# Transposing the attention's probabilities with VectorE and a pass through HBM instead of with TensorE

## The chip, the core and the metric

The kernel runs on one core of a Trainium2 chip. The core has a matrix engine (TensorE, PE in the profile, with its weight loads as PEld), three engines for elementwise work (VectorE or DVE, ScalarE or ACT, GpSimd or POOL), a queue that issues transfers (SyncE or SP) and 16 DMA engines that move data between HBM and the on-chip memory SBUF. SBUF has 128 partitions. TensorE writes to a second memory, PSUM, which has eight banks of 128 x 512 fp32. The metric is the device time of one execution in microseconds, lower is better.

## The reference: what is computed

One decoder block on 512 positions of 1024 channels, in fp32. A combined projection feeds a gated short convolution and an attention; both are merged with two gates, projected and added to the input; a gated FFN with a convolution follows.

```
h   = rmsnorm(x);  P = h @ w_in
yA  = B * causal_dwconv3(C * x_in)
yB  = attention(q, compressed / selected / window keys)     # 8 heads of 64, 2 key groups
x   = x + ( sigmoid(gA) * (yA @ W_A) + sigmoid(gB) * (yB @ W_B) ) @ W_o
x   = x + ( silu(conv3(W_g rmsnorm(x)) + b) * (W_u rmsnorm(x)) ) @ W_down
```

The attention is what matters here. For a block of 128 queries, each head has three softmaxes: over at most 31 compressed keys, over the selected blocks and over a window. With 512 positions there are 8 blocks of 64 keys and up to 16 may be selected, so all are; the window is 512 long. The last two are thus both plain causal attention, over different keys and values:

```
p   = softmax(where(key <= query, q . k * scale, -1e30))
out = g0 * (p_cmp @ v_cmp) + g1 * (p_sel @ v_sel) + g2 * (p_win @ v_win)
```

## The kernel before

All products run in a fast fp32 form (F32R) that keeps fewer bits, so each factor is split into a high and a low part, and a product takes three matmuls (high x high, high x low, low x high). `dense` (lines 408 to 414) does this for the weight tiles: one tile of 128 output channels takes 8 x 3 matmuls of 128x512.

The stages are: the token projections (q, keys, values), the heads (norm and rotary embedding), the compressed keys, the attention, then the convolution tiles `conv_tile` (12 weight tiles, PSUM name pa), the gate tiles `gate_tile` (16, pg), the mixing of the convolution `mix_a_pair` (pma), the mixing of the attention (pmb), the output projection w_o, and the FFN. A planner puts the instructions of each engine in an order of its own, by a timeline that it works out ahead of the run from dependencies, program order and its own costs. What depends on nothing in the attention (pa, pg, pma) is therefore mixed into it. The order of each engine and of each DMA queue is fixed by the time the kernel runs; each instruction waits for its inputs and its buffers.

The attention is `attend(pt_, g, qt)`, lines 595 to 708, called for the query tiles 3, 2, 1, 0 and the groups 0, 1 (lines 789 to 791). Query tile qt sees qt + 1 key tiles of 128. Per branch (br 1 is the window, br 0 the selected keys) and for four heads:

- Two matmuls give the scores of a head, 128 queries on the partitions, keys along the row (lines 608, 609). VectorE adds the causal mask to the last tile (657) and takes the negated maximum (658). ScalarE writes the exponential to `e` and sums it (659).
- VectorE makes 1/sum times the branch's gate (612, 613), and ScalarE scales the four rows of `e` by it (663). For query tile 0 both branches share one `e`, and one VectorE instruction scales it (644).
- The product with the values needs the keys on the partitions. For each key tile, TensorE transposes four 128x128 squares of `e`, one per head, into a PSUM bank `pt` (687). ScalarE rounds the bank to its high part `ph` (690), VectorE subtracts to the low part `pl` (691), and two matmuls add to the accumulator `po` (693, 698).
- With br 0 come the compressed keys: their small softmax (667 to 676, two steps of it on GpSimd, 672 and 673), two transposes (679) and two matmuls (697).
- The accumulator is read out (700, 705), split in two and stored for pmb (707, 708).

A branch of a group and query tile, or for query tile 0 both branches together, is called a turn below; there are 14. The buffers: three tiles `e` of 128x2048 (NE), three each of `ph` and `pl` (NPT), two PSUM banks for `pt`, one for `po`.

Weights come by transfers on the queue of SP, into rings. For pg and pma, `load_w` (lines 125 to 137) loads a raw tile (wr, three buffers), ScalarE makes the high part (134) and GpSimd the low part (136). The attention's tiles lie in pools that are closed after it (802); the pool for the weights of pmb takes their place (805), so the loads of w_bo (172) wait for the attention's end.

Of the kernel before, what the change touches and what calls it, by code (L numbers as in the profile page):

```python
# [18 lines left out]
P = 128  # L19
D = 1024  # L20
S = 512
# [25 lines left out]
NWF = 3  # L47
NE = 3
NWU = 11
QT_ORDER = (3, 2, 1, 0)  # L50
NPT = 3
NF_T = 10
# [30 lines left out]
def tile_block(ctx: ExitStack, tc: tile.TileContext, xT, pos, par, par2, w_tok, w_a3, w_gate, w_ao, w_bo, w_o,  # L83
               w_ff, w_dn, c_w1, out):
    nc = tc.nc
    sb = ctx.enter_context(tc.tile_pool(name="sb", bufs=1, side="left"))
    ps = ctx.enter_context(tc.tile_pool(name="ps", bufs=1, space=bass.MemoryType.PSUM))
    pxg = ctx.enter_context(tc.tile_pool(name="pxg", bufs=1, side="left"))
# [501 lines left out]
    def y_tile(i):  # L590
        if i // 2 not in y_all:
            y_all[i // 2] = pa.tile([P, 4 * TOKC], F32R, name=f"y{i // 2}", tag=f"y{i // 2}", bufs=1)
        return y_all[i // 2][:, 4 * S * (i % 2):4 * S * (i % 2 + 1)].rearrange("p (a s) -> p a s", a=4)

    def attend(pt_, g, qt):
        nk = (qt + 1) * P
# [5 lines left out]
        def small(name, n, dt=F32):  # L602
            pool = pxg if name in ("mx1", "mx0", "sums1") else pb if name in ("sums0", "mcs") else pt_
            return pool.tile([P, HG, n], dt, name=f"{name}{tag}", tag=name, bufs=2)

        def scores(w, i, br, a, b):
# [9 lines left out]
        if off == 0:  # L616
# [5 lines left out]
            nc.vector.tensor_add(xc, xc, pcm[:, :, NC:2 * NC])  # L622
        acc = o_bank(f"po{tag}")
        if qt == 0:

            e = pt_.tile([P, HG, S], F32, name=f"e{tag}", tag="e", bufs=NE)[:, :, 0:2 * P]
            e4 = e.rearrange("p h (b k) -> p h b k", b=2)
            mx = pt_.tile([P, HG, 2], F32, name=f"mx{tag}", tag="mx", bufs=1)
            sums = small("sums", 2)
            for i in range(HG):  # L630
# [8 lines left out]
                for br in (1, 0):  # L639
                    nc.scalar.activation(e4[:, i, br], dg[:, br], AF.Exp, bias=mx[:, i, br:br + 1],  # L640
                                         accum_out=sums[:, i, br:br + 1])
            nc.vector.reciprocal(sums, sums)
            nc.vector.tensor_mul(sums, sums, gates[:, :, 1:3])
            nc.vector.tensor_tensor(e4, e4, sums[:, :, :, None].to_broadcast([P, HG, 2, P]), op=ALU.mult)
        for br in (1, 0):
            if qt > 0:
                o = off if br == 0 else 0
                e = pt_.tile([P, HG, S], F32, name=f"e{tag}{br}", tag="e", bufs=NE)
                mx = small(f"mx{br}", 1)
                sums = small(f"sums{br}", 1)  # L650
                for i in range(HG):
                    sc = s_bank(f"sc{tag}{i}{br}")
                    scores(sc[:, 0:o + nk], i, br, NC - o, NC + nk)
                    if o:
                        nc.vector.tensor_add(xc[:, i, :], sc[:, 0:NC], cm_add[:, qt, :])
                    dg = sc[:, o + nk - P:o + nk]
                    nc.vector.tensor_add(dg, dg, causal)
                    nc.vector.tensor_reduce(mx[:, i], sc[:, o:o + nk], axis=AX.X, op=ALU.max, negate=True)
                    nc.scalar.activation(e[:, i, 0:nk], sc[:, o:o + nk], AF.Exp, bias=mx[:, i], accum_out=sums[:, i])
                scale_of(sums, 1 + br)  # L660
                for i in range(HG):
                    v = e[:, i, 0:nk]
                    nc.scalar.activation(v, v, AF.Copy, scale=sums[:, i])
            if br == 0:
                mcs = small("mcs", 2)
# [18 lines left out]
            for kt in range(qt + 1):  # L684
                pt = t_bank(f"pt{tag}{kt}{br}")
                for i in range(HG):
                    nc.tensor.transpose(pt[:, i * P:(i + 1) * P], e[:, i, (kt + k0) * P:(kt + k0 + 1) * P], ident)  # L687
# [3 lines left out]
                nc.vector.tensor_sub(pl, pt, ph.bitcast(F32))  # L691
                w = v_t[:, kt, 2 * br + g, :]
                nc.tensor.matmul(acc, w, ph, start=kt == 0 and br == 1, stop=False)
                if kt == 0 and br == 0:
                    a4 = acc.rearrange("p (a b t) -> p a b t", a=2, b=2)
                    for b in range(2):
                        nc.tensor.matmul(a4[:, :, b], vc_t[:, b, g, :], pc, start=False, stop=False)
                nc.tensor.matmul(acc, w, pl, start=False, stop=kt == qt and br == 0)
# [3 lines left out]
        av = acc[0:HD, :].rearrange("p (a b t) -> p a b t", a=2, b=2)  # L702
        tv = tmp.rearrange("p (a b t) -> p a b t", a=2, b=2)
        for b in range(2):
            nc.vector.tensor_add(yo[b * HD:(b + 1) * HD], av[:, :, b], tv[:, :, b])
        dst = (slice(None), slice(2 * g, 2 * g + 2), slice(qt * P, (qt + 1) * P))
# [408 lines left out]
```

## Time and profile before

| | before |
|---|---|
| time, median of 3 runs | 715.41 us (715.29 to 715.93) |
| span of the profiled execution | 714.2 us |
| TensorE busy | 708.6 us (99%) |
| VectorE busy | 534.4 us (75%) |
| ScalarE busy | 432.2 us (61%) |
| GpSimd busy | 181.7 us (25%) |
| moved by DMA | 105.47 MB in 41142 packets |
| HBM written | 2.10 MB |

The span is the time from the first to the last instruction of one profiled execution; it lies 1.2 us below the median of the runs, which stands for what lies around it. In the rows, "L687" is line 687 of the kernel, followed by the engine, the operation, and output<-input by the program's names. In a group's row, "x160" is how many instructions it has; times are busy us and the mean in ns. In a timeline's row the first number is the start in us and the second the duration. The idle time of an engine that is not the bound costs nothing. The queue q1 carries SP's transfers, q0 GpSimd's and q10 ScalarE's.

### The profile page before, as it was taken

What the parts mean: (1) busy time and instruction counts of PE and PEld (TensorE: products, weight loads), DVE (VectorE), ACT (ScalarE), POOL (GpSimd) and SP (SyncE); (2) the same over time, 40 slices, a digit from 0 to 9 for tenths busy, and PEclk for the clock granted to TensorE, in tenths of its full rate; (3) what the DMA queues carried; (4) which work ended last, traced back from release to release, by engine and by line L of the source; (5) the groups of instructions that cost most, each with busy time, mean ns of one, the idle gap of its engine ahead of it and who ended that gap; (6) DMA issues with size and microseconds to landing.
All of it is one profiled execution on the core that took longest, in us unless ns stands there. A gap on an engine that the chain in (4) does not pass through costs nothing.

```text
span 714.2 us, 11374 instructions
## 1 busy us (share of the span) xinstructions
PE 708.6 (99%) x4285; PEld 633.7 (89%) x4285; DVE 534.4 (75%) x956; ACT 432.2 (61%) x722; POOL 181.7 (25%) x179
## 2 busy tenths in 40 slices
PE   9999999999999999999999999999999999999997
PEld 9999878888888888888889999899999999999986
DVE  6887886687566878366795899988787877878643
ACT  7535655967667676522676767566555765646440
POOL 3051332133433334433012220221211222111110
PEclk9999999999999999999999999999999999999999
DMA  8333677611111122335286798987978778785575
GB/s 273 98 95 118 171 177 166 136 61 59 60 63 57 60 66 83 118 124 200 90 208 129 175 231 201 226 202 187 216 179 213 173 186 199 189 200 105 123 140 150
DMA packets 41142, 105.47 MB, mean 148 GB/s; under 512 B 3968, under 2 KB 9216, under 8 KB 41088
## 3 DMA queue, kind: packets, MB, share of 16 engines
q1 hardware_dynamic: 26528, 70.41, 29.9%
q0 software_dynamic: 14272, 34.08, 27.7%
q8 instruction: 33, 0.54, 0.3%
q10 hardware_dynamic: 288, 0.26, 0.1%
q14 instruction: 21, 0.17, 0.1%
HBM read 102.64 MB, written 2.10 MB: 147 GB/s over the span
## 4 chain that ended last, share of the span: by engine, by line
PE 97%; DMA 2%; DVE 0%; ACT 0%; POOL 0%; ACTq 0%; issue 0%
PE p L412 9%; PE p L411 9%; PE p L414 9%; PE pdn L412 6%; PE pdn L411 6%; PE pdn L414 6%; PE pg L412 4%; PE pg L411 4%; PE pg L414 4%; PE pa L414 3%; PE pa L411 3%; PE pa L412 3%; PE pt L687 2%; PE po L411 2%; PE po L412 2%; PE po L414 2%
## 5 line engine op out<-in xcount | busy, mean ns | idle before, releaser
L412 PE MATMUL p<-xf_l,sh 128*128 128x256 f32 x336 | 80.6, 277 | 0.0
L411 PE MATMUL p<-xf_h,sh 128*128 128x256 f32 x336 | 80.5, 277 | 0.0
L412 PE MATMUL pdn<-al,wh_d 128*128 128x512 f32 x176 | 68.7, 391 | 0.0
L153 ACT ACTIVATE sh<-s 128x1024 fp32r<-128x1024 f32 x44 | 46.2, 1057 | 37.1 <-PE p L412 24.8
L411 PE MATMUL pdn<-ah,wh_d 128*128 128x512 f32 x176 | 68.5, 390 | 0.0
L412 PEld LDWEIGHTS p<-xf_l,sh 128*128 128x128 f32 x336 | 63.0, 188 | 0.1
L411 PEld LDWEIGHTS p<-xf_h,sh 128*128 128x128 f32 x336 | 63.0, 188 | 0.1
L161 POOL DMA_DIRECT2D wl_s<-in_w_ff_dram x22 | 19.5, 885 | 167.0 <-ACT wl_s L160 156.0
L154 DVE TENSOR_TENSOR sl<-s,sh 128x1024 fp32r<-128x1024 f32 x44 | 53.5, 1218 | 8.7 <-ACT sh L153 8.7
L159 ACT ACTIVATE wh_s<-wr_s 128x1024 fp32r<-128x1024 f32 x22 | 23.3, 1058 | 53.5 <-PE pdn L412 50.6
L414 PE MATMUL p<-xf_h,sl 128*128 128x256 f32 x336 | 51.5, 277 | 0.0
L136 POOL TENSOR_TENSOR wl_g<-wr_g,wh_g 128x1024 fp32r<-128x1024 f32 x16 | 38.4, 2400 | 50.8 <-ACT wh_g L134 25.4
L411 PE MATMUL pg<-xg_h,wh_g 128*128 128x512 f32 x128 | 50.7, 396 | 0.0
L412 PE MATMUL pg<-xg_l,wh_g 128*128 128x512 f32 x128 | 50.6, 395 | 0.0
L414 PE MATMUL pdn<-ah,wl_d 128*128 128x512 f32 x176 | 47.7, 389 | 0.0
L161 POOL DMA_DIRECT2D wl_d<-in_w_dn_dram x22 | 26.5, 1203 | 76.9 <-ACT wl_d L160 70.2
L1034 DVE TENSOR_TENSOR x<-x,pdn 128x512 f32<-128x512 f32 x48 | 32.7, 682 | 16.3 <-PE pdn L414 15.6
L414 PEld LDWEIGHTS p<-xf_h,sl 128*128 128x128 f32 x336 | 44.5, 188 | 0.2
L411 PE MATMUL p<-xf_h,wh_s 128*128 128x256 f32 x168 | 40.5, 276 | 0.0
L412 PE MATMUL p<-xf_l,wh_s 128*128 128x256 f32 x168 | 40.5, 276 | 0.0
L414 PEld LDWEIGHTS pdn<-ah,wl_d 128*128 128x128 f32 x176 | 33.0, 188 | 6.9
L412 PEld LDWEIGHTS pdn<-al,wh_d 128*128 128x128 f32 x176 | 33.0, 188 | 6.2
(361 smaller groups left out, 2119.9 us busy)
## 6 DMA issues: line engine op xcount, KB each, us to landing
wr_s<-in_w_ff_dram SPq DMA_DIRECT2D x44, 512.0 KB, 4.8
wl_s<-in_w_ff_dram POOLq DMA_DIRECT2D x22, 512.0 KB, 7.3
wr_d<-in_w_dn_dram SPq DMA_DIRECT2D x22, 512.0 KB, 6.1
wl_d<-in_w_dn_dram POOLq DMA_DIRECT2D x22, 512.0 KB, 8.7
wr_g<-in_w_gate_dram SPq DMA_DIRECT2D x16, 512.0 KB, 3.4
wr_a<-in_w_a_dram SPq DMA_DIRECT2D x12, 512.0 KB, 4.0
tl<-in_w_ff_dram POOLq DMA_DIRECT2D x22, 256.0 KB, 7.2
wl_a<-in_w_a_dram POOLq DMA_DIRECT2D x10, 512.0 KB, 7.8
```

Source lines behind the costliest of these rows:

```text
L136: e.tensor_sub(lo[:, 0:n], raw[:, 0:n], hi[:, 0:n].bitcast(F32))
L153: hi = nc.scalar.activation(h, v, AF.Copy)
L154: nc.vector.tensor_sub(l, v, h.bitcast(F32))
L159: nc.scalar.activation(h, raw, AF.Copy)
L161: nc.gpsimd.dma_start(l if dst is None else dst, src, accum_op=ALU.add)
L411: nc.tensor.matmul(acc, wh, xh, start=first and i == 0, stop=False)
L412: nc.tensor.matmul(acc, wh, xl, start=False, stop=False)
L414: nc.tensor.matmul(acc, wl, xh, start=False, stop=last and i == len(units) - 1)
L687: nc.tensor.transpose(pt[:, i * P:(i + 1) * P], e[:, i, (kt + k0) * P:(kt + k0 + 1) * P], ident)
L1034: nc.vector.tensor_add(xj, xj, acc)
```

## The change

The exponentials are written to `e` in another order: for each block of 32 keys, the four heads side by side, 32 values each (`e_tile`, `squares`). In that order, `turn` does for a whole turn what the transposes of line 687 did:

1. One VectorE instruction transposes every square of 32 by 32 of `e` in place. Within a square, keys are then on the partitions and queries along the row, but a square of the queries 32a to 32a+31 still stands on the partitions 32a to 32a+31, and the key blocks along the row.
2. Four transfers on SP's queue, one for each a, store the squares to a scratch tensor in HBM.
3. A fifth transfer on the same queue loads them into `tn`, with the 32-key block of a key tile setting the partitions and a the place in the row.

A row of 128 floats (four heads of 32 queries) is what stays contiguous in both transfers. The columns of `po` are then in the order (a, head, query) instead of (head, query); `by_head` takes them apart where the compressed keys are added and where `po` is read out. The loop over the key tiles takes `pl` from `tn` instead of from PSUM: ScalarE rounds it to `ph`, and VectorE subtracts in place. For query tile 0, two VectorE instructions scale `e`, one for each branch.

The rings: `e` has two buffers instead of three, `ph` two instead of three, `pl` none of its own, `tn` two of 128x2048.

```diff
-NE = 3
+NE = 2
-NPT = 3
+NPT = 2
+NTN = 2
+SQ = 32
+QB = P // SQ
...
+    dr = ctx.enter_context(tc.tile_pool(name="dr", bufs=1, space=bass.MemoryType.DRAM))
...
+    def squares(v):
+        return v.rearrange("p (b i) -> p b i", i=SQ)
+
+    def by_head(v, b):
+        return v.rearrange("p (q a b i) -> p a b q i", q=QB, a=2, b=2)[:, :, b]
...
+        def e_tile(name):
+            return pt_.tile([P, S // SQ, HG, SQ], F32, name=name, tag="e", bufs=NE)
+
+        def turn(e, n):
+            v = e[:, 0:n * QB].rearrange("p b h i -> p (b h i)")
+            nc.vector.transpose(v, v)
+            v = v.rearrange("p (b r) -> p b r", r=P)
+            mid = dr.tile([QB, n, QB, SQ, P], F32, name=f"td_{e.name}", tag=f"td_{e.name}", bufs=1)
+            for a in range(QB):
+                nc.sync.dma_start(mid[a].rearrange("k b j r -> j (k b) r"), v[a * SQ:(a + 1) * SQ])
+            dst = pt_.tile([P, NT * QB, P], F32R, name=f"tn_{e.name}", tag="tn", bufs=NTN)[:, 0:n * QB]
+            nc.sync.dma_start(dst.bitcast(F32), mid.rearrange("a k b j r -> (b j) (a k) r"))
+            return dst.rearrange("p (a k) r -> p k a r", k=n)
...
-            nc.vector.tensor_tensor(e4, e4, sums[:, :, :, None].to_broadcast([P, HG, 2, P]), op=ALU.mult)
+            for br in (1, 0):
+                nc.vector.tensor_tensor(e4(br), e4(br), sums[:, None, :, br:br + 1].to_broadcast([P, QB, HG, SQ]), op=ALU.mult)
+            turned = turn(e, 2)
...
-                    nc.scalar.activation(e[:, i, 0:nk], sc[:, o:o + nk], AF.Exp, bias=mx[:, i], accum_out=sums[:, i])
+                    nc.scalar.activation(e[:, 0:nk // SQ, i], squares(sc[:, o:o + nk]), AF.Exp, bias=mx[:, i],
+                                         accum_out=sums[:, i])
...
+                turned = turn(e, qt + 1)
...
-                pt = t_bank(f"pt{tag}{kt}{br}")
-                for i in range(HG):
-                    nc.tensor.transpose(pt[:, i * P:(i + 1) * P], e[:, i, (kt + k0) * P:(kt + k0 + 1) * P], ident)
-                ph = pt_.tile([P, 512], F32R, name=f"ph{tag}{kt}{br}", tag="pth", bufs=NPT)
-                pl = pt_.tile([P, 512], F32R, name=f"pl{tag}{kt}{br}", tag="ptl", bufs=NPT)
+                pl = turned[:, kt + k0]
+                pt = pl.bitcast(F32)
+                ph = pt_.tile([P, QB, P], F32R, name=f"ph{tag}{kt}{br}", tag="pth", bufs=NPT)
                 nc.scalar.activation(ph, pt, AF.Copy)
                 nc.vector.tensor_sub(pl, pt, ph.bitcast(F32))
...
-                nc.tensor.matmul(acc, w, ph, start=kt == 0 and br == 1, stop=False)
+                nc.tensor.matmul(acc4, w, ph, start=kt == 0 and br == 1, stop=False)
...
-                        nc.tensor.matmul(a4[:, :, b], vc_t[:, b, g, :], pc, start=False, stop=False)
+                        nc.tensor.matmul(by_head(acc, b), vc_t[:, b, g, :], pc.rearrange("p a (q i) -> p a q i", i=SQ),
+                                         start=False, stop=False)
-                nc.tensor.matmul(acc, w, pl, start=False, stop=kt == qt and br == 0)
+                nc.tensor.matmul(acc4, w, pl, start=False, stop=kt == qt and br == 0)
```

More of the change, by code (lines that the diff above doesn't have):

```diff
@@ L623, in attend @@
         acc = o_bank(f"po{tag}")
+        acc4 = acc.rearrange("p (a r) -> p a r", a=QB)
         if qt == 0:
-            e = pt_.tile([P, HG, S], F32, name=f"e{tag}", tag="e", bufs=NE)[:, :, 0:2 * P]
-            e4 = e.rearrange("p h (b k) -> p h b k", b=2)
+            e = e_tile(f"e{tag}")
+            e4 = lambda br: e[:, br * QB:(br + 1) * QB]
             mx = pt_.tile([P, HG, 2], F32, name=f"mx{tag}", tag="mx", bufs=1)
@@ L639, in attend @@
                 for br in (1, 0):
-                    nc.scalar.activation(e4[:, i, br], dg[:, br], AF.Exp, bias=mx[:, i, br:br + 1],
+                    nc.scalar.activation(e4(br)[:, :, i], squares(dg[:, br]), AF.Exp, bias=mx[:, i, br:br + 1],
                                          accum_out=sums[:, i, br:br + 1])
@@ L647, in attend @@
                 o = off if br == 0 else 0
-                e = pt_.tile([P, HG, S], F32, name=f"e{tag}{br}", tag="e", bufs=NE)
+                e = e_tile(f"e{tag}{br}")
                 mx = small(f"mx{br}", 1)
@@ L658, in attend @@
                     nc.vector.tensor_reduce(mx[:, i], sc[:, o:o + nk], axis=AX.X, op=ALU.max, negate=True)
-                    nc.scalar.activation(e[:, i, 0:nk], sc[:, o:o + nk], AF.Exp, bias=mx[:, i], accum_out=sums[:, i])
+                    nc.scalar.activation(e[:, 0:nk // SQ, i], squares(sc[:, o:o + nk]), AF.Exp, bias=mx[:, i],
+                                         accum_out=sums[:, i])
                 scale_of(sums, 1 + br)
                 for i in range(HG):
-                    v = e[:, i, 0:nk]
+                    v = e[:, 0:nk // SQ, i]
                     nc.scalar.activation(v, v, AF.Copy, scale=sums[:, i])
+                turned = turn(e, qt + 1)
             if br == 0:
@@ L692, in attend @@
                 w = v_t[:, kt, 2 * br + g, :]
-                nc.tensor.matmul(acc, w, ph, start=kt == 0 and br == 1, stop=False)
+                nc.tensor.matmul(acc4, w, ph, start=kt == 0 and br == 1, stop=False)
                 if kt == 0 and br == 0:
-                    a4 = acc.rearrange("p (a b t) -> p a b t", a=2, b=2)
                     for b in range(2):
-                        nc.tensor.matmul(a4[:, :, b], vc_t[:, b, g, :], pc, start=False, stop=False)
-                nc.tensor.matmul(acc, w, pl, start=False, stop=kt == qt and br == 0)
+                        nc.tensor.matmul(by_head(acc, b), vc_t[:, b, g, :], pc.rearrange("p a (q i) -> p a q i", i=SQ),
+                                         start=False, stop=False)
+                nc.tensor.matmul(acc4, w, pl, start=False, stop=kt == qt and br == 0)
         tmp = pt_.tile([HD, 512], F32, name=f"yt{tag}", tag="yt", bufs=1)
@@ L701, in attend @@
         yo = pt_.tile([P, 2, P], F32, name=f"yo{tag}", tag="yo", bufs=1)
-        av = acc[0:HD, :].rearrange("p (a b t) -> p a b t", a=2, b=2)
-        tv = tmp.rearrange("p (a b t) -> p a b t", a=2, b=2)
         for b in range(2):
-            nc.vector.tensor_add(yo[b * HD:(b + 1) * HD], av[:, :, b], tv[:, :, b])
+            nc.vector.tensor_add(yo[b * HD:(b + 1) * HD].rearrange("p a (q i) -> p a q i", i=SQ), by_head(acc[0:HD], b),
+                                 by_head(tmp, b))
         dst = (slice(None), slice(2 * g, 2 * g + 2), slice(qt * P, (qt + 1) * P))
```

## The prediction, made before the changed kernel was run

> **What bounds the kernel now.** I read the page's busy shares and its chain of waits first, then the chain's shares by line.
>
> ```profile
> span 714.2 us, 11374 instructions
> ...
> PE 708.6 (99%) x4285; PEld 633.7 (89%) x4285; DVE 534.4 (75%) x956; ACT 432.2 (61%) x722; POOL 181.7 (25%) x179
> ...
> PE 97%; DMA 2%; DVE 0%; ACT 0%; POOL 0%; ACTq 0%; issue 0%
> ...
> by line: PE p L412 9.5%; PE p L411 9.4%; PE p L414 9.4%; PE pdn L412 5.6%; PE pdn L411 5.6%; PE pdn L414 5.6%; PE pg L412 4.1%; PE pg L411 4.1%; PE pg L414 4.1%; PE pa L414 2.9%; PE pa L411 2.6%; PE pa L412 2.6%; PE pt L687 2.4%; PE po L411
> ...
> L687 PE MATMUL pt<-ident,e x160: 270/272/274, 131.8 to 290.3; 128*128 128x128 f32 x160
> ```
>
> TensorE is the bound, everywhere: 97% of the chain. The 160 transposes that the change removes are 2.4% of it, 17.1 us, or 107 ns each (their 272 ns overlap). That is the most the change can give. They run from 131.8 to 290.3 us, inside the attention, so I then asked the stretches for each engine's load there, beside the FFN stretch, where the core is fullest.
>
> ```profile
> core 0: us, PE busy (x) PEld busy (x) DVE busy (x) ACT busy (x) POOL busy (x), PEclk, DMA share, GB/s
> 114.00:296.40 182.40, 182.40 (x927) 153.36 (x926) 126.73 (x309) 127.71 (x295) 64.49 (x49) 1.00 0.26 74
> 400.00:500.00 100.00, 100.00 (x752) 95.08 (x751) 91.59 (x129) 69.75 (x94) 20.24 (x21) 1.00 0.85 204
> ```
>
> The columns are TensorE, its weight loads, VectorE, ScalarE and GpSimd. In the attention TensorE is never idle, because the matmuls of the conv, gate and mixing tiles (pa, pg, pma) fill the waits of the attention. VectorE is 69% busy and the DMA engines 26%. The FFN stretch shows that TensorE can be full beside a VectorE at 92% and DMA at 85%.
>
> **How much of the 17.1 us can come out.** The attention's end is a second bound. The output projection pmb needs all heads, and its weights wait for the memory that the attention frees. These rows are the tail, and the gate matmuls left after it:
>
> ```profile
> 296.16 0.40 PE L698 MATMUL po<-pl,v_t 128*128 128x512 f32 x1
> 296.64 1.75 SPq L172 DMA_DIRECT2D wr_bo<-in_w_bo_dram  x4
> 300.24 1.06 ACT L153 ACTIVATE wh_bo<-wr_bo 128x1024 fp32r<-128x1024 f32 x1 [1.08 <-DMA wr_bo<-in_w_bo_dram]
> 304.57 0.39 PE L411 MATMUL pmb<-y,wh_bo 128*128 128x512 f32 x1
> ...
> 296.40:338.30 41.90, 14.48 (x61) 11.26 (x60) 2.05 (x3) 1.00 0.54 186
> ```
>
> The last row is the stretch after the last value matmul for pg alone: 14.5 us of gate work is left. From the end of that matmul (296.56) to the split weights (301.30) are 4.7 us that need cover. So 9.8 us of gate work is spare. Let d be how much later (or earlier) the last value matmul comes than now. TensorE has 17.1 us less to do, and it can bring forward no more than the spare gates, so the gain is min(17.1, 9.8 - d). With the attention ending where it does now, 9.8 us; the whole 17.1 only if it ends 7.3 us earlier; nothing if it ends 9.8 us later. All the rest is the size of d.
>
> **What sets the attention's pace now.**
>
> ```profile
> 161.85 0.27 PE L687 MATMUL pt<-ident,e 128*128 128x128 f32 x1
> 162.65 0.58 ACT L659 ACTIVATE e<-sc,mx 128x384 f32<-128x384 f32 x1
> 172.93 2.13 ACT L663 ACTIVATE e<-e,sums 128x384 f32<-128x384 f32 x4 [1.00 <-DVE sums L613]
> 175.98 0.60 PE L687 MATMUL pt<-ident,e 128*128 128x128 f32 x4
> 177.11 0.58 ACT L659 ACTIVATE e<-sc,mx 128x384 f32<-128x384 f32 x1
> ```
>
> The exponentials of a turn (one query tile, group and branch; 14 in all) begin within about a microsecond of the last transpose of the turn three before: the ring of three e buffers is the pace. Turns start 14.5 us apart here, so a buffer is held for some 43 us, although it is scaled 12.4 us after its first exponential.
>
> **The change part by part: the round trip.** Each turn is now one VectorE transpose, four stores, one load. Prices:
>
> ```profile
> q10 hardware_dynamic: 156, 0.08, 16.2%
> ...
> wr_g<-in_w_gate_dram SPq DMA_DIRECT2D x16, 512.0 KB, 3.4
> ...
> out_dram<-x SPq DMA_DIRECT2D x8, 256.0 KB, 2.0
> ...
> L154 DVE TENSOR_TENSOR sl<-s,sh 128x1024 fp32r<-128x1024 f32 x44 | 53.5, 1218 | 8.7 <-ACT sh L153 8.7
> L691 DVE TENSOR_TENSOR pl<-pt,ph x40: 674/687/694, 135.1 to 291.3; 128x512 fp32r<-128x512 f32 x40
> ```
>
> VectorE: 512 more elements cost 1218 - 687 = 531 ns, so 1.04 ns each and 0.15 us to start. A transpose of 512 n elements (n key tiles) is then 0.68, 1.22, 1.75 and 2.28 us for n = 1 to 4. The changed kernel transposes 40 key tiles in 14 instructions: 40 x 0.531 + 14 x 0.15 = 23.4 us. The trace has no VectorE transpose; twice as slow per element would be 45 us, and as a lower end half of it, 12 us. I take 23.4, since an element of such an instruction is what the rows price. [...]
>
> DMA: the run of the moved tensors is 128 floats, 512 bytes. The first DMA row is the queue of the par load in a window of 2.1 us (1.9 to 4.0 us): 156 packets of 0.08 MB, 513 bytes each, took 16.2% of 16 engines, so 0.162 x 16 x 2.1 / 156 = 35 ns a packet. A turn stores 512 n packets and loads as many: 2048 x 35 / 16 = 4.5 us each way for n = 4, 2.2 for n = 2. The fixed part: the attention's stretch moves 74 GB/s at 26%, so 285 at full share; of the 3.4 us of a 512 KB load 1.8 are data and 1.6 fixed, of the 2.0 us of an output store 0.9 and 1.1. The round trip is 1.1 + 4.5 + 1.6 + 4.5 = 11.7 us for n = 4, some 14 with the transpose. All turns: 40 x 1024 packets x 35 / 16 = 90 us of the 16 engines. With the 47 us (26% of 182.4) there now that is 137 of 182 us, 75%, under the 85% of the FFN stretch. Bounds: at the 285 GB/s of the attention's larger packets a packet of 512 bytes is 29 ns, 73 us in all; at twice the 35 ns the DMA engines would be the bound, at 227 us. I keep 35, since that row has the very size.
>
> **What hides it.** The latency of a turn hides behind other turns as long as the rings turn fast enough. NE falls to 2, but an e buffer is now free when its stores land: 12.4 + 1.75 + 1.1 + 3.4 = 18.6 us after the first exponential for n = 3, 9.3 a turn with two buffers, against 14.5 now. The tn ring (2) is held by a load of 6.1 us and four value steps; at 0.7 us of VectorE a step it is under 10 us, 5 a turn. So neither ring slows the pace, and without that cover each of the 14 turns would show up to 14 us. Five DMAs a turn wait at the head of SP's queue: the first store for VectorE, the load for the stores (up to 5.6 us). Behind them stand the weight loads (wr_g, wr_ao), and behind those ScalarE's and GpSimd's splits and the pg matmuls.
>
> ```profile
> SPq L130 <- POOL wl_g L136: 109.1, 13, 10.6
> ```
>
> These loads already wait 8.4 us each for GpSimd to free a buffer and land in 3.4, three tiles deep, so 6 us more costs nothing. The reverse is a danger: a store behind a load that is still waiting. ScalarE's split reads SBUF in place of PSUM, and the scaling of qt 0 becomes two instructions of half the size; ScalarE is 30% idle, VectorE pays 0.3 us for the latter. The orders of the head columns cost no instruction.
>
> **VectorE is the next bound.** This is where I see the price. L691 reads pt from PSUM now, flat at 674 to 694 ns. In the changed kernel both of its inputs are in SBUF. Rows of such an instruction beside GpSimd:
>
> ```profile
> 279.32 2.40 POOL L136 TENSOR_TENSOR wl_g<-wr_g,wh_g 128x1024 fp32r<-128x1024 f32 x1
> 279.62 2.11 DVE L613 TENSOR_TENSOR mcs<-mcs,gate_n 128x4 f32<-128x4 f32 x1
> ...
> L613 DVE TENSOR_TENSOR mcs<-mcs,gate_n x8: 166/918/2111, 127.9 to 279.6; 128x4 f32<-128x4 f32 x8
> ```
>
> Four elements take 166 ns alone and 2.11 us where GpSimd is at work, and end as it ends (281.72). GpSimd is busy 64.5 of 182.4 us, 35%: 14 of the 40 splits should meet it and wait about half of its 2.4 us, 1.1 us, so 15 us. [...] Without this wait the term is nothing.
>
> VectorE in the attention: 126.7 + 23.4 + 15 = 165 us. At the 92% that it bears in the FFN stretch this takes 180 us, against 182.4 now: d = -2. The tail by itself: in
>
> ```profile
> 277.82 1.21 DVE L644 TENSOR_TENSOR e<-e,sums 128x1024 f32<-128x1024 f32 x1
> ```
>
> the last turn is scaled by 279.03; then 0.2 (second scaling) + 1.2 (transpose) + 3.3 (store) + 3.8 (load) and 4 us of splits and matmuls end at 291.5, 5 us before 296.56. Against both stands that the attention's instructions depend on one another more than the FFN's. I take d = 0.
>
> **The sum.** 714.2 - 9.8 = 704.4 us of span; the median of the runs is 1.2 above this execution's span, so 705.6.
>
> **The rivals.** *Whole gain*: the freed e ring lets the attention end 7.3 us or more earlier; 715.4 - 17.1 = 698.3. For it: the 9.3 against 14.5 us a turn. Against: VectorE would have to do its 165 us in 175, 94%.
> *VectorE is late* (slower): VectorE waits 55.7 us (182.4 - 126.7) in the attention now. If two thirds of these remain beside 165 us of work, it takes 202 us, d = 20 and 9.8 - 20 = -10: 725.6. It decides from 27 us of kept waits on. For it: DVE is in order, and a transpose of 2.28 us stands before others' reductions.
> *The landing is late in TensorE's order* (slower): the order on each queue is fixed by a planner before the run, so a value matmul placed too early holds the gates behind it. At 2 us for each of 14 turns TensorE idles 28 us: 17.1 - 28 = -11, 726.3. It decides from 1.2 us a turn on. Against: TensorE hardly waits for DMA now, but for 512-byte runs the trace shows no such case.
> *No change*: any of the two at half its size, d near 10.
>
> **How the numbers follow.** Forecast 0.37 (own range 700 to 712), whole gain 0.13, no change 0.09, VectorE late 0.21, landing late 0.20. The runs before lie within 0.1%; 0.2%, 1.4 us, is about what this kernel's measurement tells from no change. Faster 0.50, same 0.09, slower 0.41. The range is 697.5 to 728: from the whole gain to a little over the two slower cases' prices.
>
> **What would show it.** TensorE's L687 gone and its busy time 17 us less; in its waits, idle time before L693 and L698 released by a tn load or by DVE pl would be the rivals, and its size decides. VectorE's transpose near 2.28 us for 2048 elements; L691 with a maximum near 3 us; stores' and loads' time to landing near 3 to 6 us; wr_bo issued near 296 us. I am wrong in kind if the last value matmul comes after 306 us, or if DMA's share in the attention passes 85%.

## The result, and the profile after

The changed kernel takes 720.8 us (median of 5 runs, 717.6 to 721.0), the kernel before 715.4: a ratio of 1.006, 95% interval 1.0043 to 1.0078. It is 0.6% slower; forecast were 705.6 us and a gain. The profiled execution took 720.8 us with a span of 719.1, against 714.2 before. First the page's busy shares and its chain of waits.

```profile
span 719.1 us, 11240 instructions
...
PE 700.3 (97%) x4125; PEld 619.9 (86%) x4125; DVE 562.7 (78%) x972; ACT 432.8 (60%) x722; POOL 184.0 (26%) x179
...
PE 81%; DVE 9%; DMA 4%; ACT 3%; issue 1%; SPq 1%; POOL 0%; ACTq 0%; DVEq 0%
```

TensorE has 160 instructions less, but its busy time fell by 8.3 us only, and its idle time (span less busy) rose from 5.6 to 18.8 us: 13.2 - 8.3 = 4.9 us, the whole loss. VectorE and the DMA engines now hold 13% of the chain; TensorE holds 81% of it, where it held 97%. The three largest waits of TensorE, by line:

```profile
PE po L727 <- DVE tn_e L720: 5.3, 6, 1.5
PE pmb L415 <- ACT wh_bo L157: 3.5, 1, 3.5
PE sc L634 <- ACT e L688: 2.5, 2, 2.0
```

The columns are total, times and longest wait. The first is the value matmul that waits for VectorE's low part; the second stands at the end of the attention. The next rows are the attention up to the last value matmul, a piece of the chain of waits, and the first long wait of TensorE with what stands ahead of it:

```profile
114.00:306.80 192.80, 182.98 (x820) 147.49 (x820) 156.94 (x325) 129.22 (x297) 67.99 (x50) 0.99 0.69 179
...
134.72 11.00 DMA td_e<-e
...
145.83 0.69 ACT L688 ACTIVATE e<-sc,mx 128x512 f32<-128x512 f32 x1 [6.65 <-DMA td_e<-e]
146.66 0.50 PE L634 MATMUL sc<-kk,qT 128*128 128x512 f32 x1 [2.03 <-ACT e L688]
```

So 9.8 of the 13.2 us of new idle time lie in the attention, where TensorE had none before, and 3.5 at its end. Of the 9.8, 6.7 end with VectorE (the low parts and two smaller lines). 2.0 hang on the first turn's stores, which landed only after 11 us: the third turn's exponentials waited 6.65 us for the `e` buffer, one of two, that these stores read. The tail in order of time (start, duration):

```profile
306.39 0.40 PE L727 MATMUL po<-tn_e,v_t 128*128 128x512 f32 x1
306.87 1.78 SPq L176 DMA_DIRECT2D wr_bo<-in_w_bo_dram  x4
310.56 1.06 ACT L157 ACTIVATE wh_bo<-wr_bo 128x1024 fp32r<-128x1024 f32 x1 [0.74 <-DMA wr_bo<-in_w_bo_dram]
311.67 0.80 PE L415 MATMUL pmb<-y,wh_bo 128*128 128x512 f32 x1 [3.50 <-ACT wh_bo L157]
```

The last value matmul starts at 306.39, where it started at 296.16: d = +10.2 us. The gates that covered the load of the output projection's weights are used up by then, and TensorE sits idle for 3.5 us. A third cost is in the granted clock. These stretches are the one of that idle time and the one after it, and the same pair about the first long wait of the attention; the columns are those of the prediction's stretches:

```profile
143.74:147.15 3.41, 1.38 (x6) 0.84 (x6) 1.69 (x4) 1.32 (x4) 1.26 (x1) 1.00 0.33 120
147.15:150.56 3.41, 3.41 (x10) 2.68 (x9) 0.00 (x0) 1.07 (x4) 0.00 (x0) 0.50 0.90 253
307.58:310.99 3.41, 0.59 (x3) 0.17 (x1) 1.52 (x3) 1.48 (x3) 0.72 (x1) 1.00 0.91 290
310.99:317.82 6.83, 6.15 (x15) 4.81 (x16) 3.67 (x3) 2.74 (x3) 0.00 (x0) 0.50 1.02 359
```

After a stretch in which TensorE was busy 1.38 of 3.41 us the clock stands at half for 3.41 us; after one with 0.59 of 3.41, for 6.83. Half a clock for 10.24 us is up to 5.1 us of work lost, 1.7 of them in the attention and 3.4 behind it. Before, the clock was 1.00 over the whole attention.

What VectorE does in the attention, by shape (busy time, mean ns of one), and what the stretches say of it and of the DMA engines:

```profile
L720 DVE TENSOR_TENSOR tn_e<-tn_e,ph 128x512 fp32r<-128x512 f32 x40 | 42.7, 1070 | 15.2 <-ACT ph L719 14.9
L623 DVE STREAM_TRANSPOSE e<-e 128x2048 f32<-128x2048 f32 x4 | 9.2, 2301 | 1.4 <-ACT e L693 1.4
L623 DVE STREAM_TRANSPOSE e<-e 128x1024 f32<-128x1024 f32 x6 | 7.4, 1238 | 2.7 <-ACT e L693 2.7
L623 DVE STREAM_TRANSPOSE e<-e 128x1536 f32<-128x1536 f32 x4 | 7.1, 1773 | 2.5 <-ACT e L693 2.5
...
114.00:296.40 182.40, 172.58 (x772) 138.83 (x772) 153.10 (x320) 125.17 (x290) 64.16 (x47) 0.99 0.73 188
```

The transposes cost 23.7 us. The subtraction costs 42.7, where 40 times 687 ns were 27.5. A place near the end shows how the two go together, VectorE first and GpSimd's row last:

```profile
273.29 1.56 DVE L672 TENSOR_TENSOR e<-e,sums 128x512 f32<-128x512 f32 x2
274.77 2.89 DVE L720 TENSOR_TENSOR tn_e<-tn_e,ph 128x512 fp32r<-128x512 f32 x1
277.58 0.17 DVE L638 RECIPROCAL mcs<-mcs 128x4 f32<-128x4 f32 x1
277.66 0.15 DVE L662 TENSOR_TENSOR xc<-sc,cm_add 128x32 f32<-128x32 f32 x1
277.74 0.68 DVE L779 TENSOR_TENSOR t_all<-pg,rb_n 128x512 f32<-128x512 f32 x1
278.34 1.23 DVE L623 STREAM_TRANSPOSE e<-e 128x1024 f32<-128x1024 f32 x1
...
274.26 2.85 POOL L140 TENSOR_TENSOR wl_g<-wr_g,wh_g 128x1024 fp32r<-128x1024 f32 x1
```

The last turn but one is scaled by 274.85 and could be transposed at once. The transposition starts at 278.34, behind a subtraction of 2.89 us beside GpSimd's low part of a weight (GpSimd ends at 277.11, the subtraction at 277.66) and three short instructions. The last turn then comes by its round trip:

```profile
289.85 2.13 SPq L627 DMA_DIRECT2D td_e<-e  x4
293.89 0.38 SPq L629 DMA_DIRECT2D tn_e<-td_e  x1
...
298.39 1.15 ACT L719 ACTIVATE ph<-tn_e 128x512 fp32r<-128x512 f32 x2 [0.83 <-PE po L722]
```

It was transposed by 289.77; the first split starts 8.6 us later. (The row puts the last 0.83 us of that down to a `ph` buffer, one of two, that a matmul still read.) TensorE didn't stand idle for it:

```profile
292.00:306.87 14.87, 14.87 (x69) 12.29 (x70) 6.95 (x13) 7.88 (x15) 4.23 (x4) 1.00 0.21 55
```

The last split ended at 300.96. The turn's value matmuls begin at 305.48, because TensorE's order has gates in front of them.

### The profile page after: what moved, and what is told of

Read it like the earlier page. It is cut to its first block, busy times and chain, and to the rows that moved or that the text cites. A ratio compares the mean times of both kernels' runs of the same rounds, so it can differ in the third digit from the quotient of the medians.

```text
span 719.1 us, 11240 instructions
## 1 busy us (share of the span) xinstructions
PE 700.3 (97%) x4125; PEld 619.9 (86%) x4125; DVE 562.7 (78%) x972; ACT 432.8 (60%) x722; POOL 184.0 (26%) x179
## 3 DMA queue, kind: packets, MB, share of 16 engines
q0 software_dynamic: 14272, 34.08, 27.5%
## 4 chain that ended last, share of the span: by engine, by line
PE 81%; DVE 9%; DMA 4%; ACT 3%; issue 1%; SPq 1%; POOL 0%; ACTq 0%; DVEq 0%
PE p L416 9%; PE p L415 9%; PE p L418 9%; PE pdn L416 6%; PE pdn L415 6%; PE pdn L418 6%; DVE tn_e L720 3%; PE pa L418 2%; PE pg L416 2%; PE pg L415 2%; PE pg L418 2%; DMA td_e<-e 2%; PE po L415 2%; PE po L416 2%; PE po L418 2%; DVE e L623 2%
## 5 line engine op out<-in xcount | busy, mean ns | idle before, releaser
L720 DVE TENSOR_TENSOR tn_e<-tn_e,ph 128x512 fp32r<-128x512 f32 x40 | 42.7, 1070 | 15.2 <-ACT ph L719 14.9
L688 ACT ACTIVATE e<-sc,mx 128x512 f32<-128x512 f32 (+2 forms) x48 | 27.5, 576 | 21.4 <-DVE mx L687 12.7
```

What stands on the lines that cost most here:

```text
L688: nc.scalar.activation(e[:, 0:nk // SQ, i], squares(sc[:, o:o + nk]), AF.Exp, bias=mx[:, i], accum_out=sums[:, i])
```

## The experiments

Two theories stood against each other: VectorE is late (the transposes, and the subtraction that waits for GpSimd), and the landing is late (the way through HBM). Each kernel's order on the queues is planned anew before its run, so two kernels differ a little in more than their edit: one of them below has the same VectorE work as another, more transfers, and is 3.8 us faster. A difference of 4 us or less between two of my kernels is therefore not read as a price by itself. Every time below is a median; a ratio is that to the kernel before on the same chip.

**One part of the change at a time.** The first kernel is that of before without its transposes, the second has VectorE's transposes but no way through HBM. Both keep the rings of the kernel before (three `e`, three `ph`), where the changed kernel has two of each. The core of the diffs against the kernel before:

```
...
-                    nc.tensor.transpose(pt[:, i * P:(i + 1) * P], e[:, i, (kt + k0) * P:(kt + k0 + 1) * P], ident)
+                pt = e[:, :, (kt + k0) * P:(kt + k0 + 1) * P]
```

and in the second kernel besides

```
+            nc.vector.transpose(e, e)
...
+                for v in (e[:, :, 0:nk],):
+                    nc.vector.transpose(v, v)
```

> The kernel before with its 160 transposes left out: the splits read the scaled e tile where it lies (so the value products are those of an untransposed matrix; the transposition is left out). The 17.1 us of TensorE work are gone, nothing takes their place but the low-part subtraction, which now has both inputs in SBUF. If VectorE's meeting with GpSimd (15.4 us more on the subtraction in the changed kernel) is enough to eat the gain, this kernel shows it alone: 712 to 716 us. If it is the landing that eats it, nothing lands here, and the kernel takes 698 to 702 us.

> The same, with the VectorE transposes done in place on the e tile, and no store and no load (the 32 by 32 squares stay where they are: the putting in place is left out). All of the changed kernel's VectorE work is there, 23 us of transposes and the meeting with GpSimd, but no way through HBM. If VectorE is what is late: 717 to 722 us, as the changed kernel. If the landing is: 700 to 707 us, and the 14 to 20 us between this kernel and the changed one are the price of the way through HBM.

Without transposes: 698.0 us, ratio 0.9747 (0.9733 to 0.9762). The whole 17.1 us come out, though the subtraction meets GpSimd in this kernel too. With VectorE's transposes: 709.1 us, 0.9909 (0.9887 to 0.993). So VectorE's transposes cost 11.1 us, and the way through HBM with its smaller rings the other 11.7. Each theory had expected one price; the 709.1 lie between the two expectations, and there are two prices of about equal size.

**The waits for GpSimd, taken away.** GpSimd's low parts of the gate and mixing weights are left out, in the kernel before (as a control), in the changed one and in the one with the transposes alone.

```
-            e = nc.gpsimd if by == "pool" else nc.vector
-            e.tensor_sub(lo[:, 0:n], raw[:, 0:n], hi[:, 0:n].bitcast(F32))
+            if by == "pool":
+                return hi, hi
+            nc.vector.tensor_sub(lo[:, 0:n], raw[:, 0:n], hi[:, 0:n].bitcast(F32))
```

> The kernel before, with GpSimd's low-part subtractions of the weights left out (the high part is used twice): a control for the next run. TensorE has the same matmuls and is full, so both theories expect 713 to 716 us.

> The changed kernel with the same GpSimd subtractions left out (the weights' high part is used twice): no GpSimd read meets the splits, so the 40 subtractions should fall from 1070 to about 690 ns each, 15 us less for VectorE in the attention. If VectorE is what is late: 705 to 710 us, faster than its control. If the landing is: 718 to 721 us, the distance to its control stays at 4 to 6 us.

> The kernel with the VectorE transposes in place and no way through HBM (709.1 us), now with GpSimd's low-part subtractions of the gate and mixing weights left out too (the high part is used twice). It splits the 11.1 us that the transposes cost there. The 40 subtractions fall from 945 to about 690 ns, 10 us less of VectorE. If it is the sum of VectorE's work that makes it late, 698 to 702 us, the whole gain. If it is the place of the transposes in VectorE's order (up to 2.3 us before others' reductions), 706 to 709 us.

The control: 715.75 us, 1.0001 (0.999 to 1.0012), so where TensorE is full the edit by itself does nothing. The changed kernel without GpSimd's low parts comes out between its two expectations. The times side by side, in us:

```
                                 GpSimd's low parts made    left out
no transposes, no way               698.0                      -
VectorE's transposes, no way        709.1                    698.3
the same and the way through HBM    720.8                    713.8
```

The transposes alone are free (698.3 beside 698.0), and the waits for GpSimd alone are free (698.0 has them: its 40 subtractions took 953 ns each). Together they cost 10.9 us. The subtraction's rows in the two kernels of the middle line, with GpSimd's low parts and without:

```profile
L693 DVE TENSOR_TENSOR pl<-e,ph 128x512 fp32r<-128x512 f32 x40 | 37.4, 945 | 3.4 <-ACT ph L692 2.8 <-PE po L700 0.4
```

```profile
L694 DVE TENSOR_TENSOR pl<-e,ph 128x512 fp32r<-128x512 f32 x40 | 26.8, 683 | 3.2 <-ACT e L666 1.7 <-ACT ph L693 0.6 <-PE po L701 0.4
```

10.6 us of VectorE's time made 10.9 us of the kernel's. The transposes are still in VectorE's order, and their price is gone: it is the sum of VectorE's work that counts, as the first of the two expectations had it. The way through HBM costs 15.6 us where nothing waits for GpSimd and 11.7 where it does: the two prices overlap by 4, which is within the scatter between kernels. The subtraction has both inputs in SBUF in these two kernels and took 945 ns beside GpSimd's low parts, 683 without them; by what way GpSimd holds it up is not shown.

What the 11.7 us consist of can be read from the profiled executions (span, idle time of TensorE, time at half clock, all us):

```
                                span    idle   half clock
no transposes                  696.0     5.6       0
VectorE's transposes           707.5    13.1       0
changed                        719.1    18.8     10.2
changed, low parts left out    709.9    15.6      3.4
```

From the second row to the third, 5.7 of 11.6 us are idle time and up to 5.1 are half clock.

**Traffic or latency.** Here the kernel with the transposes alone sends as many packets of 512 bytes as the round trip, and no split waits for them (an `e` buffer, one of three, is still free only when its stores are done).

```
+    def put_away(e, n):
+        for c in range(2):
...
+            for h in range(4):
+                nc.sync.dma_start(mid[h].rearrange("k p r -> p k r"), e[:, h].rearrange("p (k r) -> p k r", r=P))
...
+                put_away(e[:, :, 0:nk], qt + 1)
```

> The same kernel (709.1 us) with eight stores a turn of the transposed tile to HBM, in packets of 512 bytes, that nobody reads: as many packets, bytes and VectorE work as in the changed kernel, but no splits that wait for a landing. If the traffic itself costs (DMA engines 0.7 busy, weights later): 715 to 721 us. If it is the wait for the landing: 708 to 711 us.

705.35 us, 0.9858 (0.9843 to 0.9873): under both expectations, and no dearer than without the traffic, at a DMA share of 0.68 in the attention (0.73 in the changed kernel). So the 11.7 us are not the traffic. What is left is the landing's latency together with the smaller rings; no kernel here has the smaller rings alone, so these two are not told apart. The next two change the latency in the changed kernel: three small stores in a chain ahead of each load, and one buffer moved from the landing's ring (tn) to the e ring.

```
+            for _ in range(NTINY):
+                nc.sync.dma_start(mid[0, 0, 0, 0:1], v[0:1, 0])
```

```
-NE = 2
-NTN = 2
+NE = 3
+NTN = 1
```

> The changed kernel with three stores of 512 bytes in a row between a turn's stores and its load, each waiting for the one before (they write again what the first store wrote): every landing comes some 3 x 2 = 6 us later, with hardly any traffic, and the e buffer is held as much longer. If a landing is paid once, at the end (and in part at the start), 6 to 9 us slower: 727 to 730 us. If it is paid in every turn through the rings of two, 6 us x 14 / 2 = 42 us slower: over 740 us. If it is hidden: 721 us.

> The changed kernel with three e buffers and one tn buffer instead of two and two, the same memory. A load can then start only when the turn before has finished its value steps, so each landing of 4.1 to 6.8 us stands bare in the chain of turns. If the landing is hidden by the tn ring in the changed kernel, this shows what it hides: 14 x 4 to 6 us of it less what TensorE's gates cover, 735 us or more. If it was the e ring that held the turns back, 715 to 719 us.

The small stores: 724.7 us, ratio 1.0114 (1.0093 to 1.0136), 3.9 more than the changed kernel and between two of the expectations. They overlapped with the large ones and delayed less than I had meant. These are the last turn's rows on SP's queue:

```profile
296.13 1.85 SPq L628 DMA_DIRECT2D td_e<-e  x4
298.22 3.20 SPq L630 DMA_DIRECT2D td_e<-e  x3
302.31 0.38 SPq L632 DMA_DIRECT2D tn_e<-td_e  x1
```

6.2 us from first store to load, against 4.0 in the changed kernel: 2.1 us more a landing. Paid in every turn by rings of two that would be 2.1 x 14 / 2 = 15 us, paid once 2.1. Measured are 3.9, within the scatter of the second and far from the first. With one tn buffer (and three e buffers): 765.4 us, 1.0694 (1.0676 to 1.0712). Its largest wait of TensorE:

```profile
PE po L722 <- ACT ph L719: 39.0, 10, 5.9
```

This kernel is 44.6 us slower than the changed one, so the second tn buffer hides much. It isn't a price of each turn: ten splits hold TensorE up, and six of these waits, of 4.6 to 5.9 us, lie behind 306 us, where no gates are left and the clock stands at half for 51 us. The tn ring of two does its work; what it leaves bare is, by the run before, not one landing in every second turn.

**Another way for the same bytes.** Straight from SBUF to SBUF in 16 transfers a turn; and the weights' loads issued by GpSimd, so that SP serves the probabilities alone.

```
-            for a in range(QB):
-                nc.sync.dma_start(mid[a].rearrange("k b j r -> j (k b) r"), v[a * SQ:(a + 1) * SQ])
...
+            v = v.rearrange("p (k b) r -> p k b r", b=QB)
+            for a in range(QB):
+                for b in range(QB):
+                    nc.sync.dma_start(dst[b * SQ:(b + 1) * SQ, a * n:(a + 1) * n].bitcast(F32), v[a * SQ:(a + 1) * SQ, :, b])
```

```
-        nc.sync.dma_start(raw[:, 0:n], src)
+        (nc.gpsimd if by == "pool" else nc.sync).dma_start(raw[:, 0:n], src)
```

> The changed kernel with the way through HBM replaced by 16 transfers per turn straight from the e tile to the tn tile in SBUF: half the 512-byte packets, no load that waits for four stores at the head of SP's queue. VectorE's work is the same. The kernel with the transposes alone (709.1 us) stands 11.7 us under the changed one; if that is the landing's latency and SP's queue, this kernel takes back at least half of it: 711 to 715 us. If the landing is hidden and VectorE late alone, it stays at 719 to 722 us.

> The changed kernel with the 20 loads of the gate and mixing weights issued by GpSimd instead of SP, so that SP's queue holds only the stores and loads of the probabilities from 130 us on. If standing behind each other in SP's queue is what makes the landing late, 715 to 718 us. If it is the way itself and VectorE, 720 to 722 us; and GpSimd's issues, 0.9 us each, could make it later by some us.

The straight way: 735.9 us, 1.0281 (1.0266 to 1.0297), where I had expected a gain. SP's issues from 239.5 to 299.7 us (minimum, median and maximum ns):

```profile
L629 SPq DMA_DIRECT2D tn_e<-e x79: 585/595/1634, 239.5 to 299.7; - x79
...
DMA to landing us min/median/max: 1.9/1.9/4.8
```

Each lands in 1.9 us, but 16 issues of 0.6 us are 9.5 us of SP a turn. It put an issue time in place of a landing; TensorE's three largest waits are 11.0 (for splits), 7.9 and 7.5 us, and the clock stands at half for 34 us. The weights' loads by GpSimd: 726.4 us, 1.015 (1.0135 to 1.0165), 5.6 slower. SP's queue order is not shown to be a cause by this, nor cleared: GpSimd's issues of 20 loads now stand in its own order, beside its splits.

**The low parts by transfers instead of by GpSimd.** Nothing is left out here; the waits for GpSimd are gone by other means. The second kernel has the straight way in SBUF besides.

```
-        w = load_w(w_gate[j], D, f"g{j}", by="pool")
+        w = load_w(w_gate[j], D, f"g{j}", by="dma")
```

> The changed kernel with the low parts of the gate and mixing weights made as those of the conv weights are (two ScalarE copies and an adding transfer from HBM) instead of by GpSimd. Nothing is left out. The subtractions of the probabilities then meet no GpSimd read and should take 690 ns, as in the kernel that leaves the low parts out (713.8 us). ScalarE gets 20 x 1.06 = 21 us and the DMA engines some 10 MB more. If VectorE's meeting with GpSimd is what costs 7 us, 713 to 716 us; if the DMA engines (0.73 busy) are as near their bound as VectorE, 719 us or more.

> Both: the straight way in SBUF and the weights' low parts by transfers. If the two causes are apart, their gains add: 704 to 709 us, faster than the kernel before. If one cause shows in both, it is no better than the better of the two.

739.0 us, 1.0322 (1.0278 to 1.0365), and 760.6, 1.0636 (1.0621 to 1.0652). The attention's stretch and the landing of the large stores in the first of them:

```profile
114.00:296.40 182.40, 166.83 (x732) 133.90 (x731) 122.42 (x297) 135.15 (x295) 32.68 (x44) 0.97 0.92 230
...
td_e<-e SPq DMA_DIRECT2D x16, 256.0 KB, 9.5
```

The subtractions fall to 683 ns, as meant, and the DMA engines rise from 0.73 to 0.92; a large store that landed in 5.0 us (median of 16) takes 9.5. The weights land later as well (the gate weights after 7.4 us instead of 4.5, medians), and the mean granted clock of the profiled execution is 0.985 instead of 0.993. So the loss is more than VectorE saves; which of these landings holds the kernel up is not shown. The second kernel, meant to gain from both, is slower than either edit alone; that SP's issues come on top there is my reading, not shown.

**VectorE relieved.** All or every second of the 40 subtractions on GpSimd:

```
-                nc.vector.tensor_sub(pl, pt, ph.bitcast(F32))
+                nc.gpsimd.tensor_sub(pl, pt, ph.bitcast(F32))
```

> The changed kernel with the 40 low-part subtractions of the probabilities moved from VectorE to GpSimd: 42.7 us off VectorE, some 40 x 1.2 = 48 us on GpSimd, which is then 116 of 193 us busy. If VectorE is what is late, 712 to 716 us. If GpSimd's turn comes too late in the chain of a value matmul, or the weights' splits behind it, 722 us or more.

> The changed kernel with every second low-part subtraction of the probabilities (even key tiles: 24 of 40) on GpSimd and the others on VectorE. With all 40 on GpSimd it took 713.6 us; GpSimd then is 102 of 166 us busy and one subtraction takes 1.3 us there. If the sum of VectorE's work is what counts, halving it gives about half the 7.2 us: 716 to 718 us. If the waits on a long chain count, and the two engines now run subtractions of one turn beside each other, 711 to 713 us.

713.6 us, 0.9972 (0.996 to 0.9985), and 717.0, 1.0021 (1.0012 to 1.003): 7.2 and 3.8 us off the changed kernel, with 42.7 and 22.3 us off VectorE; half the relief gives half the gain, as expected if VectorE's sum counts, though 3.8 us are within the scatter. GpSimd itself is not what was late: with these subtractions it is busy 102 of the 166 us from 114 to 280, and the kernel is faster. The first, with the change and all its work in it, is the only one here that beats both kernels. Its subtractions on GpSimd:

```profile
L720 POOL TENSOR_TENSOR tn_e<-tn_e,ph 128x512 fp32r<-128x512 f32 x40 | 52.9, 1335 | 28.0 <-ACT ph L719 25.4 <-PE po L722 2.4
```

**The end of the attention.** TensorE transposes the two turns of query tile 0, the last ones, as before; then with the subtractions of the others on GpSimd; then with query tile 1 as well. The fourth puts matmuls into the idle time before the output projection.

```
+BY_PE = (0,)
...
+        te = qt in BY_PE
...
+                if te:
+                    for i in range(HG):
+                        nc.tensor.transpose(pt[:, i], te_e[:, i, (kt + k0) * P:(kt + k0 + 1) * P], ident)
```

```
+                if g == G - 1 and qt == QT_ORDER[-1] and br == 0 and kt == qt:
+                    fill = s_bank("fill")
+                    for i in range(NFILL):
+                        m = nc.tensor.matmul(fill, w, ph, start=True, stop=True)
+                        behind(m, pv)
```

> The changed kernel, with the two turns of query tile 0, the last ones of the attention, transposed by TensorE as before (16 transposes, 1.7 us of TensorE); the other 12 go by VectorE and HBM. In the changed kernel 8.6 us pass from the last VectorE transpose to the first split, against 0.1 us where nothing lands. If the round trip is paid once, at the end, 8.6 us of it come out, less 1.7: 713 to 716 us. If it is paid at every turn by the two buffers of each ring, 12 of 14 turns still pay: 718 to 721 us.

> The same with the 36 low-part subtractions of the other 12 turns moved from VectorE to GpSimd, which alone took 7.2 us off the changed kernel (713.6). If the end's landing and VectorE's work are two separate prices, both come out: 705 to 710 us. If the second is only covered by the first, 712 to 714 us.

> The same with the four turns of query tile 1 on TensorE as well, so that only the eight largest turns (28 of 40 key tiles) go by VectorE and HBM, and TensorE does 48 transposes, 5.1 us. If the end is still the bound with only the last two turns taken out, this is 1 to 4 us faster than the kernel above; if not, 3 us slower, by TensorE's work.

> The changed kernel with 14 matmuls, whose result nobody reads, put behind the last value matmul, where TensorE sits idle 3.5 us for the output projection's weights and the granted clock then stands at half for 6.8 us. If the idle gap is what takes the clock down, the half clock after it goes and 2 to 4 us with it: 717 to 719 us. If the clock falls for another reason, 720 to 722 us.

717.8 us, 1.0022 (1.0012 to 1.0033): 3.0 faster than the changed kernel, within the scatter, and between the two expectations. Its weights for the output projection are issued at 306.3, hardly before the changed kernel's 306.9: the splits of the turn ahead of the last two, which still comes through HBM, begin at 283.8 (286.7 in the changed kernel), and TensorE's order has the last two behind it. Of 3.1 us less span up to 1.7 are half clock (6.8 us at half clock instead of 10.2). 715.5 us, 1.0001 (0.9988 to 1.0014), is no faster than with the subtractions moved alone and above both expectations, so the two gains don't add. 724.3 us, 1.0117 (1.0098 to 1.0136), is slower than both expectations: TensorE waits 7.0 us for the output projection's weights, and the clock stands at half for 17.1 us. A tile that TensorE transposes keeps its e buffer up to the value steps; that this makes it late is likely and not shown. None of the three finds the end's landing as a price of its own, which agrees with a TensorE that is busy throughout that landing.

The matmuls in the gap: 722.1 us, 1.0101 (1.0078 to 1.0125), no gain. They read a tile in the memory that the output projection's weights wait for, so they pushed the weights' load to 309.1 us, and an idle gap of 3.65 us stood behind them. This run settles nothing about the clock.

## Why the prediction was wrong, by its own steps

**The gain by the spare gates: held.** The rule was min(17.1, 9.8 - d) with d the shift of the last value matmul. Below, d is read from the issue of the output projection's weights (296.64 before), and the half clock is half of the time that the profiled execution spent at it; all in us of span.

```
kernel                            issue     d     rule   half clock   measured gain
no transposes                     276.8  -19.8   17.1      0           18.2
transposes, low parts left out    285.2  -11.4   17.1      0           17.5
transposes and traffic            294.5   -2.1   11.9      0           10.3
transposes                        297.5    0.9    8.9      0            6.7
changed, low parts left out       299.0    2.4    7.4      1.7          4.3
changed, subtractions on GpSimd   302.5    5.9    3.9      1.7          1.1
changed                           306.9   10.2   -0.4      5.1         -4.9
```

Rule less half clock is within 2.2 us of the measurement in every row. It doesn't hold for kernels that wait much longer at the end: for the straight way in SBUF (issue at 319.5) it gives -30 where -20 was measured; that much of the half clock there falls on idle time is my reading, not shown. So the working was right up to d for the kernels of the table, and d is where it fell.

**d = 0: the step that failed.** It measured +10.2, by two of its parts.

*"At the 92% that it bears in the FFN stretch this takes 180 us."* The two new terms were right: 23.4 us of transposes (23.7 measured), 15 us of waits for GpSimd (42.7 - 27.5 = 15.2). The sum with VectorE's other work was not: 165 us were forecast, and 156.9 were measured even up to 306.8 us, among other things because the 20 small products of line 613 (639 in the changed kernel) met GpSimd less, 6.1 us instead of 13.8. The 92% was wrong: in the changed kernel VectorE is busy for 81% of the attention (156.94 of 192.80 us), and TensorE already waits 6.7 us for it. The FFN stretch is no measure for the attention, whose chain goes through VectorE several times a turn, in VectorE's order (the last turn but one shows a scaled tile that stands 3.5 us). From 114 to 280 us VectorE is busy 135.59 of 166 us, 82%, in the kernel of 698.3 us, and 146.33, 88%, in that of 709.1. The first is free; 6% more come out in full.

*"So neither ring slows the pace", and with it that a landing "hides behind other turns".* For the tn ring it held on the whole. For the e ring it failed at the start: the working has the stores of a large turn land 5.6 us after their issue (1.1 + 4.5), and the first turn's took 11, beside weight loads, with the DMA engines at 0.88 (130 to 143.74 us). The third turn's exponentials waited 6.65 us for that buffer, TensorE 2.03, and half a clock for 3.41 us came behind it. At the end the account was off in another way. The working has a landing of 3.3 + 3.8 us there, against 8.6 measured from transposition to split, and sets it on a scaling at 279.03, the time of before; the last scaling now ends about 288. But that landing cost no idle time: after the splits of 301.0 the last value matmuls come at 305.5 to 306.4, where TensorE's order, written before the run, has gates in front of them, and these gates are then missing as cover. The round trip with its smaller rings costs 11.7 to 15.6 us together, by the times side by side; how much of that is the start, the rings, the end or the order in between the runs don't tell apart.

*The half clock* was not in the prediction at all: up to 5.1 us in the profiled execution. 1.7 of them fall in the attention, where they may be in d already; 3.4 come on top of the rule's -0.4. It doesn't explain the whole loss: the one of the five timed executions that kept the full clock took 717.6 us, 3.2 less than the median and still 2.2 more than the kernel before.

**What else held.** The DMA engines' share in the attention, 75% forecast, is 0.73; traffic alone cost nothing (705.35 us with it, 709.1 without). In the kernel with the low parts by transfers the share is 0.92, and a large store takes 9.5 us instead of 5.0. "6 us more costs nothing", for SP's queue, has no run for or against it. TensorE's work fell by the 160 instructions, but its busy time by 8.3 us instead of 17.1; up to 5.1 of the difference are the half clock. The rest, 3.7, is about what the kernel with VectorE's transposes shows without any half clock (694.4 busy, against 690.4 with no transposes); why TensorE's busy time grows where it waits is not shown.

**The rivals.** "VectorE is late" and "the landing is late" were priced at 725.6 and 726.3, one or the other. Both came, at 7.0 to 10.9 and 11.7 to 15.6 us, and what they took was 22.8 us of a gain of 17.4. I had forecast the case in which neither did.

## What to carry to other kernels

Where an engine is the bound over many stages, price a move off it by the two things that it disturbs: the in-order engine that takes it (add its waits, and see whether they stand on the chain), and the new latency at the start, where a ring holds little yet and other transfers stand in its way (here 2.0 us of waiting and 3.41 us at half clock after it). Ask as well where the inputs of the instructions left behind now lie: here a subtraction of VectorE took 687 ns with one input in PSUM and 1070 with both in SBUF, each time with GpSimd's low parts made beside it, and 682 with both in SBUF and those left out; moving it to GpSimd gave 7.2 us. And leave spare work behind the last wait: once the cover was used up, a gap of 3.5 us was followed by 6.8 us at half clock, up to another 3.4.

## What the runs showed of the hardware beside this

The granted clock fell to half after less idle time than I had thought to look for. In the changed kernel a wait of 2.03 us (within a stretch with TensorE busy 1.38 of 3.41 us) was followed by 3.41 us at half clock; a wait of 3.50 us by 6.83, twice that. These two stretches of half clock begin at 147.15 and 310.99 us, 163.84 us apart, 48 times the 3.413 us that the first lasts. In the kernel with the end transposed by TensorE, a stretch with TensorE busy 1.81 of 3.40 us (176.0 to 179.4) was followed by 3.40 us at 0.50, and a wait of 3.01 us before the output projection (busy 0.01 of 3.00 us, 307.8 to 310.8) by 7.20 us at 1.00. So in these runs the length of a gap alone does not decide; what does is not shown. In the kernel with one tn buffer, where TensorE went on waiting, the clock stayed down for 51.20 us:

```profile
310.44:361.64 51.20, 20.48 (x45) 12.89 (x46) 14.69 (x23) 15.27 (x26) 2.90 (x4) 0.50 0.43 139
```

The second: a store's issue was not always short. The four stores of the first turn took SP 5.50 us to issue, those of the last 2.13:

```profile
131.54 5.50 SPq L627 DMA_DIRECT2D td_e<-e  x4
```
